# First stage of a two-layer diffusion backbone: block 3's shift formed on TensorE, small loads issued by ScalarE, products of zeros in two early waits of TensorE

## The chip, the cores and the metric

The kernel runs on one core of one Trainium2 chip. The time is the device time of one execution in microseconds (us). Of the kernel before, three runs are given, and one more execution was recorded by the profiler. The core's engines are named as the profile names them: PE (TensorE, matrix products), DVE (VectorE), ACT (ScalarE), POOL (GpSimd) and SP (SyncE, which only issues loads). Each takes its instructions in the order of the program and waits for others by semaphores.

## The reference, cut to what matters

A latent stream of 256 tokens and a context of 256 tokens, both 2048 wide, go through two layers; the change touches the beginning of the first, in which the input is modulated and keys and values are formed:

```python
sh1, sc1, g1, sh2, sc2, g2 = ada_params(c[:, None, :], ada_w[i], ada_b[i])   # silu(c) @ ada_w + ada_b, six parts
a = modulate(h, sh1, sc1)                                                     # h * (1 + sc1) + sh1
csh1, csc1, ... = ada_params(c_ctx, ada_w[i], ada_b[i])                       # the same for the context
ac = modulate(hc, csh1, csc1)
...
q, k, v = jnp.split(a @ w_qkv, 3, axis=-1)
```

So scale and shift, 2048 numbers each for latent and for context, are themselves products of a vector with a 2048 x 2048 matrix, and they are needed before the first product of the layer. All is fp32.

## The kernel before

The 2048 channels are cut into 16 **blocks** of 128 (`kt` in the code). In the first stage a loop over the blocks (functions `fetch`, `dot`, `gather`, `modulate`, `keys`, `values`) does for each block: load its two 128 x 2048 pieces of the modulation matrix (1 MB each: scale, then shift), its 128 x 512 of the transposed input (`xt`) and its 896 columns of key and value weights (`rkv`); form scale and shift; modulate; and add the block's share to three heads of keys (`kps`) and to 512 columns of values (`vps`), which stay in PSUM for the whole stage.

Products of data are made from two parts, a rounded high part and the rest (`hi`, `lo`; `ah`, `al` for the input): ACT rounds (L93), DVE subtracts (L94), and `mm3` issues three products for one (L88, L89, L90): high by high, high by rest, rest by high. A block has nine of them for the keys and twelve for the values. From block 3 on, twelve further ones form early shares of four more heads (`eps`).

Scale and shift come about in two ways:

- On PE (`dot`): 16 products against `c_pad`, silu of `c` and `c_ctx` in a padded tile (L350), leave four partial rows in PSUM. `gather` has ACT copy them to `row` (L359), sums and turns them by a product with the selector `sel` (L362), and DVE adds the bias `badj` and writes `mod` (L364). In the trace each of these full fp32 products has two records, so 32 for one set of 16.
- On DVE (`dot_dve`), for the shift of the blocks from `DVE0` = 3 on: the piece is laid out the other way round, and two passes over 2048 columns with sums (L337), against silu of `c` in `c_bc` and of `c_ctx` in `cc_bc` (which borrows the tile `oT`), give both shifts, to which L340 adds the bias.

`modulate` is then two scaled copies on ACT (`tmp`, L374), and the split into `ah` and `al`.

What sets the order: `pin` (`keep_in_program_order`) fixes the order in which an engine's pinned instructions are issued; the rest is placed by a scheduler. PE works ahead: within block `kt` it makes the sets of 16 of block `kt + 2` (`dots(ahead)`, after the keys) and the selection of that block after half of the values. Block 3 is an exception: its sets are made at the end of block 1, its selection within the keys of block 2 (`rows(3)`).

Loads are issued by SP (big blocks) and ACT, each in its own order. The 1 MB pieces share four buffers: three in `st` and, for the shift of every odd block, the one of `gate`. A load waits until the last reader of its buffer is done, and those behind it wait with it. Eight semaphores are shared in turn by all loads of SP and ACT, so a load also waits until the one eight before it has landed.

At the start ACT issues `badj`, `ident` and `sel`, then loads its table and makes silu of `c_col`; DVE copies that to `c_pad`; SP loads `c_col` and the two rows of `c`, which POOL spreads to all partitions (`spread`, L82), and then the blocks.

Of the kernel before, what the change touches and what calls it, by code (L numbers as in the profile page):

```python
# [11 lines left out]
F32 = mybir.dt.float32  # L12
# [7 lines left out]
P = 128  # L20
# [20 lines left out]
ADA = 4  # L41
FETCH = 3
BUSY = 0.3
DVE0 = 3
W0 = HK0 * P + 512
EARLY = tuple((3 + 4 * g + h, h, 4 * g) for g in range(3) for h in range(4))
EN = 4
# [4 lines left out]
def hybrid_kernel(ctx: ExitStack, tc: tile.TileContext, i, out):  # L52
# [3 lines left out]
    outer = ctx.enter_context(tc.tile_pool(name="outer", bufs=1))  # L56

    c_col = outer.tile([P, KT, 2], F32, tag="ccol", name="c_col")
    nc.sync.dma_start(c_col, i["c_col"])
    badj = outer.tile([P, 2, 6, KT], F32, tag="badj", name="badj")  # L60
    nc.scalar.dma_start(badj, i["ada_b_col"])
    ident = outer.tile([P, P], F32, tag="ident", name="ident")
    nc.scalar.dma_start(ident, i["ident"])
    eps_t = outer.tile([P, 1], F32, tag="eps", name="eps_t")
    nc.gpsimd.memset(eps_t, EPS)
    warm = outer.tile([P, 1], F32, tag="warm", name="warm")
    S.activation(c_col, c_col, AF.Silu)
    for t in (SC1, SC2):
        V.tensor_scalar(badj[:, :, t, :], badj[:, :, t, :], 1.0, None, ALU.add)
    lncol = outer.tile([P, 4, 2, KT], F32, tag="lncol", name="lncol")  # L70
    cols = outer.tile([P, 2, 6, KT], F32, tag="cols", name="cols")
    cols2 = outer.tile([P, 2, 6, KT], F32, tag="cols2", name="cols2")
# [7 lines left out]
    def spread(dst, src):  # L80
        nc.sync.dma_start(dst[0:1, :], src[None, :])
        nc.gpsimd.partition_broadcast(dst, dst[0:1, :])  # L82
# [194 lines left out]
    with tc.tile_pool(name="attnX", bufs=1) as px, ExitStack() as late:  # L277
# [21 lines left out]
        with tc.tile_pool(name="st", bufs=1) as st:  # L299
# [11 lines left out]
            def fetch(kt):  # L311
# [2 lines left out]
                    held[kt, t] = load_st(src, f"ap{kt}{t}", 2 * kt + t)  # L314
                load_x(kt)

            c_pad = st.tile([P, KT, 32], F32, tag="cpad", name="c_pad")
            nc.gpsimd.memset(c_pad, 0.0)
            V.tensor_copy(c_pad[:, :, 0:2], c_col)
            sel = st.tile([P, 2], F32, tag="sel", name="sel")  # L320
            nc.scalar.dma_start(sel, i["sel"])
            mod = st.tile([P, 2, KT, 2], F32, tag="mod", name="mod")
            kps = [stp_pool.tile([P, 512], F32, tag=f"k{h}", name=f"kps{h}") for h in range(HK0)]
            vps = [stp_pool.tile([P, 512], F32, tag=f"v{b}", name=f"vps{b}") for b in range(4)]
# [30 lines left out]
            def gather(kt):  # L355
                ps = dps.pop(kt)
                ts = 1 if kt >= DVE0 else 2
                row = st.tile([P, 2 * P], F32, tag="row", name=f"row{kt}", bufs=1)
                S.copy(row[:, 0 : ts * P], ps[:, 0 : ts * P])  # L359
                o = ps[:, 256:260].rearrange("p (t b) -> p t b", t=2)  # L360
                for t in range(ts):
                    pin(T.matmul(o[:, t, :], row[:, t * P : (t + 1) * P], sel, start=True, stop=True))  # L362
                for t, ada in enumerate((SC1, SH1)[:ts]):
                    V.tensor_scalar(mod[:, t, kt, :], o[:, t, :], badj[:, 0, ada, kt : kt + 1], None, ALU.add)  # L364
# [5 lines left out]
            def modulate(kt):  # L370
                tmp = st.tile([P, 512], F32, tag="tmp", name=f"tmp{kt}", bufs=2)
                for b in range(2):
                    sl = slice(b * 256, (b + 1) * 256)
                    S.activation(  # L374
                        tmp[:, sl], xt[kt][:, sl], AF.Identity,
                        bias=mod[:, 1, kt, b : b + 1], scale=mod[:, 0, kt, b : b + 1],
                    )
                split_into(ah[:, kt, :], al[:, kt, :], tmp)

            for n, bc in enumerate((c_bc, cc_bc)):  # L380
                spread(bc, i["c_rows"][n])
            fetch(0)
            prefetch(1)
            fetch(1)
            for t in range(2):
                dot(0, t)
            gather(0)
            modulate(0)
            for kt in range(KT):
                hi, lo = piece()  # L390
# [22 lines left out]
                keys(0)  # L413
                if kt == 2:
                    rows(3)
                keys(1)
                keys(2)
                dots(ahead)
# [14 lines left out]
                for at, h, k0 in EARLY:  # L433
                    if at == kt:
# [8 lines left out]
                        else:  # L443
                            free = NH - 2 * (h - HK0 + 1)
                            early[h] = oT[:, free : free + 2, :].rearrange("p a b -> p (a b)")
                            V.tensor_copy(early[h], ps)
                if 1 < kt and kt + 1 < KT:
                    modulate(kt + 1)
            nc.sync.dma_start(lncol, i["ln_col"])
        pa = late.enter_context(tc.tile_pool(name="attnA", bufs=1))  # L450
# [589 lines left out]
```

## Time and profile before

| | us |
|---|---|
| three runs: lowest, median, highest | 2460.63, 2462.59, 2463.62 |
| the profiled execution | 2464.19 |
| its span, first to last instruction | 2462.4 |
| PE, PE's weight loads, DVE, ACT, POOL busy | 2388.5, 1979.4, 1753.7, 1120.5, 110.3 |
| mean granted clock of TensorE | 0.991 of full |

The profiled execution's own time is 1.8 us over its span. In the profile a line such as L350 is the line of the kernel printed above; names of tiles stand without their numbers, output before input; "x32" counts instructions of one kind that follow each other; what stands behind "<-" in square brackets is who ended the idle time before the instruction. A view of busy times can be asked for any stretch, and it gives the granted clock of TensorE for it, 1.00 or less.

### The profile page before, as it was taken

The page shows a single profiled execution, that of the slowest core. Times are in us where ns is not written, and L with a number is a line of the kernel's source. Part 1 is how long each engine was busy: PE and PEld are TensorE (multiplying, and loading weights), DVE is VectorE, ACT ScalarE, POOL GpSimd, SP SyncE. Part 2 cuts the span into 40 slices and gives each one's busy share as a digit, 9 for nine tenths or more (in the row PEclk, how much of TensorE's full clock was granted, in tenths as well). Part 3 has the DMA queues.
Part 4 walks back from the last instruction along what each step waited for, and adds up shares of the span by engine and source line. Part 5 has one row for each costly group of instructions (what it writes and reads, how often), then busy time and mean ns, then how long its engine had stood idle before and what let it go on. Part 6 is the DMA issues. An engine that isn't in the chain of part 4 may idle for free. (4 is left out here: it accounts for less than half of the span.)

```text
span 2462.4 us, 31266 instructions
## 1 busy us (share of the span) xinstructions
PE 2388.5 (97%) x11574; PEld 1979.4 (80%) x11574; DVE 1753.7 (71%) x2158; ACT 1120.5 (46%) x1534; POOL 110.3 (4%) x54
## 2 busy tenths in 40 slices
PE   7999999999999999999999999899999999999998
PEld 5788888888788888887888778777888888888886
DVE  4878877777887777666778778778755555566666
ACT  3344434335554444443455554445544444445453
POOL 0000200000010010000000010020100000020000
PEclk9999999999999999999999999999999999999999
DMA  9978787877578888887888767766567676766563
GB/s 358 346 248 266 254 288 260 273 253 246 188 241 284 293 280 299 284 290 275 280 290 283 247 208 263 241 210 196 199 229 229 226 227 225 230 198 190 178 211 131
DMA packets 167682, 610.63 MB, mean 248 GB/s; under 512 B 19076, under 2 KB 21572, under 8 KB 163172
## 3 DMA queue, kind: packets, MB, share of 16 engines
q1 hardware_dynamic: 120888, 440.64, 53.9%
q10 hardware_dynamic: 46512, 167.96, 19.9%
q8 instruction: 90, 1.47, 0.2%
q14 instruction: 64, 0.52, 0.1%
q0 software_dynamic: 128, 0.03, 0.0%
HBM read 606.46 MB, written 2.10 MB: 247 GB/s over the span
## 5 line engine op out<-in xcount | busy, mean ns | idle before, releaser
L93 ACT CAST hwf<-rwf 128x1024 fp32r<-128x1024 f32 x320 | 336.9, 1053 | 491.2 <-PE pu L90 206.0
L94 DVE TENSOR_TENSOR lwf<-rwf,hwf 128x1024 fp32r<-128x1024 f32 x320 | 404.3, 1277 | 173.8 <-ACT hwf L93 172.8
L152 DVE SCALAR_TENSOR_TENSOR ad<-ad,c_bc 128x1024 f32<-128x1024 f32 x192 | 234.0, 1222 | 168.9 <-DMA ad<-in_ada_t 168.3
L88 PE MATMUL pod<-hwd,ghd 128*128 128x512 f32 x684 | 267.3, 391 | 3.5 <-DVE sg L815 3.5
L90 PE MATMUL pod<-hwd,gld 128*128 128x512 f32 x684 | 266.5, 390 | 0.7 <-DVE gld L94 0.7
L89 PE MATMUL pod<-lwd,ghd 128*128 128x512 f32 x684 | 266.8, 390 | 0.0
L176 DVE SCALAR_TENSOR_TENSOR gate<-ag,c_col,gate 128x1024 f32<-128x1024 f32 x128 | 164.4, 1288 | 121.1 <-DMA ag<-in_ada_g 120.8
L94 DVE TENSOR_TENSOR lwd<-rwd,hwd 128x1024 fp32r<-128x1024 f32 x172 | 211.7, 1232 | 51.3 <-ACT hwd L93 51.0
L93 ACT CAST hwd<-rwd 128x1024 fp32r<-128x1024 f32 x172 | 180.3, 1049 | 33.3 <-PE pu L90 11.5
L88 PEld LDWEIGHTS pod<-hwd,ghd 128*128 128x128 f32 x684 | 128.7, 188 | 30.5 <-DVE sg L815 4.0
L90 PEld LDWEIGHTS pod<-hwd,gld 128*128 128x128 f32 x684 | 128.7, 188 | 28.1 <-DVE gld L94 1.2
L89 PEld LDWEIGHTS pod<-lwd,ghd 128*128 128x128 f32 x684 | 128.8, 188 | 26.6
L88 PE MATMUL pg<-hwf,f1h 128*128 128x512 f32 x320 | 126.4, 395 | 0.0
L88 PE MATMUL pg<-hwf,f0h 128*128 128x512 f32 x320 | 126.4, 395 | 0.0
L90 PE MATMUL pg<-hwf,f1l 128*128 128x512 f32 x320 | 124.7, 390 | 0.0
L90 PE MATMUL pg<-hwf,f0l 128*128 128x512 f32 x320 | 124.7, 390 | 0.0
L88 PE MATMUL pu<-hwf,f0h 128*128 128x512 f32 x320 | 124.5, 389 | 0.0
L89 PE MATMUL pu<-lwf,f0h 128*128 128x512 f32 x320 | 124.5, 389 | 0.0
L90 PE MATMUL pu<-hwf,f0l 128*128 128x512 f32 x320 | 124.5, 389 | 0.0
L88 PE MATMUL pu<-hwf,f1h 128*128 128x512 f32 x320 | 124.5, 389 | 0.0
L89 PE MATMUL pu<-lwf,f1h 128*128 128x512 f32 x320 | 124.5, 389 | 0.0
L90 PE MATMUL pu<-hwf,f1l 128*128 128x512 f32 x320 | 124.5, 389 | 0.0
(338 smaller groups left out, 5345.1 us busy)
## 6 DMA issues: line engine op xcount, KB each, us to landing
rwf<-in_w_in_t SPq DMA_DIRECT2D x320, 512.0 KB
ad<-in_ada_t ACTq DMA_DIRECT2D x192, 512.0 KB
rwd<-in_w_out SPq DMA_DIRECT2D x176, 512.0 KB
ag<-in_ada_g ACTq DMA_DIRECT2D x128, 512.0 KB
rwg<-in_w_gin SPq DMA_DIRECT2D x64, 512.0 KB
ap<-in_ada_p SPq DMA_DIRECT2D x19, 1024.0 KB
rwq<-in_w_q SPq DMA_DIRECT2D x32, 512.0 KB
rwo<-in_w_o SPq DMA_DIRECT2D x32, 512.0 KB
```

Of the source, the lines that this page charges most:

```text
L88: keep(T.matmul(ps, sh, mh, start=first, stop=False))
L89: keep(T.matmul(ps, sh, ml, start=False, stop=False))
L90: keep(T.matmul(ps, sl, mh, start=False, stop=last))
L93: S.copy(hi, src)
L94: V.tensor_tensor(lo, src, hi.bitcast(F32), ALU.subtract)
L152: V.scalar_tensor_tensor(r, r, 1.0, c_bc[:, half * 1024 : (half + 1) * 1024], ALU.mult, ALU.mult, accum_out=o[:, nt : nt + 1],)
L176: V.scalar_tensor_tensor(g, loaded.pop(key), c_col[:, kt, 0:1], g, ALU.mult, ALU.add)
```

## The change

`DVE0` goes from 3 to 4, so the shift of block 3 is formed on PE like those of blocks 0 to 2, from a piece that is laid out as theirs; `modulate(3)` moves from the end of block 2 to right behind block 3's selection. At the start, `sel`, the bias in two halves (one for each layer), the two rows of `c` and `ident` are issued by ACT in a fixed order, behind its table load, and silu of `c` is written to `c_pad` by ACT; SP issues only `c_col` ahead of the blocks. `heat` puts products of a tile of zeros into PE's order: two 512 wide ahead of the first set of block 0, three 256 wide behind block 0's selection. They go to a PSUM tile whose first real product starts it anew.

```diff
--- before.py
+++ after.py
@@ -41,7 +41,7 @@
 ADA = 4
 FETCH = 3
 BUSY = 0.3
-DVE0 = 3
+DVE0 = 4
 W0 = HK0 * P + 512
 EARLY = tuple((3 + 4 * g + h, h, 4 * g) for g in range(3) for h in range(4))
 EN = 4
@@ -56,17 +56,13 @@
     outer = ctx.enter_context(tc.tile_pool(name="outer", bufs=1))
 
     c_col = outer.tile([P, KT, 2], F32, tag="ccol", name="c_col")
-    nc.sync.dma_start(c_col, i["c_col"])
+    tc.keep_in_program_order(nc.sync.dma_start(c_col, i["c_col"]))
     badj = outer.tile([P, 2, 6, KT], F32, tag="badj", name="badj")
-    nc.scalar.dma_start(badj, i["ada_b_col"])
     ident = outer.tile([P, P], F32, tag="ident", name="ident")
-    nc.scalar.dma_start(ident, i["ident"])
     eps_t = outer.tile([P, 1], F32, tag="eps", name="eps_t")
     nc.gpsimd.memset(eps_t, EPS)
     warm = outer.tile([P, 1], F32, tag="warm", name="warm")
-    S.activation(c_col, c_col, AF.Silu)
-    for t in (SC1, SC2):
-        V.tensor_scalar(badj[:, :, t, :], badj[:, :, t, :], 1.0, None, ALU.add)
+    tc.keep_in_program_order(S.activation(warm, eps_t, AF.Silu))
     lncol = outer.tile([P, 4, 2, KT], F32, tag="lncol", name="lncol")
     cols = outer.tile([P, 2, 6, KT], F32, tag="cols", name="cols")
     cols2 = outer.tile([P, 2, 6, KT], F32, tag="cols2", name="cols2")
@@ -314,11 +310,15 @@
                     held[kt, t] = load_st(src, f"ap{kt}{t}", 2 * kt + t)
                 load_x(kt)
 
+            zero = st.tile([P, 512], F32, tag="zero", name="zero")
+            nc.gpsimd.memset(zero, 0.0)
             c_pad = st.tile([P, KT, 32], F32, tag="cpad", name="c_pad")
             nc.gpsimd.memset(c_pad, 0.0)
-            V.tensor_copy(c_pad[:, :, 0:2], c_col)
             sel = st.tile([P, 2], F32, tag="sel", name="sel")
-            nc.scalar.dma_start(sel, i["sel"])
+            pin(nc.scalar.dma_start(sel, i["sel"]))
+            pin(nc.scalar.dma_start(badj[:, 0], i["ada_b_col"][:, 0]))
+            pin(S.activation(c_pad[:, :, 0:2], c_col, AF.Silu))
+            pin(S.activation(c_col, c_col, AF.Silu))
             mod = st.tile([P, 2, KT, 2], F32, tag="mod", name="mod")
             kps = [stp_pool.tile([P, 512], F32, tag=f"k{h}", name=f"kps{h}") for h in range(HK0)]
             vps = [stp_pool.tile([P, 512], F32, tag=f"v{b}", name=f"vps{b}") for b in range(4)]
@@ -378,13 +378,26 @@
                 split_into(ah[:, kt, :], al[:, kt, :], tmp)
 
             for n, bc in enumerate((c_bc, cc_bc)):
-                spread(bc, i["c_rows"][n])
+                pin(nc.scalar.dma_start(bc[0:1, :], i["c_rows"][n][None, :]))
+                nc.gpsimd.partition_broadcast(bc, bc[0:1, :])
+            pin(nc.scalar.dma_start(badj[:, 1], i["ada_b_col"][:, 1]))
+            pin(nc.scalar.dma_start(ident, i["ident"]))
+            for layer in range(2):
+                for t in (SC1, SC2):
+                    V.tensor_scalar(badj[:, layer, t, :], badj[:, layer, t, :], 1.0, None, ALU.add)
+
+            def heat(n, width):
+                for _ in range(n):
+                    pin(T.matmul(vps[3][:, :width], zero[:, :P], zero[:, :width], start=True, stop=True))
+
+            heat(2, 512)
             fetch(0)
             prefetch(1)
             fetch(1)
             for t in range(2):
                 dot(0, t)
             gather(0)
+            heat(3, 256)
             modulate(0)
             for kt in range(KT):
                 hi, lo = piece()
@@ -413,6 +426,7 @@
                 keys(0)
                 if kt == 2:
                     rows(3)
+                    modulate(3)
                 keys(1)
                 keys(2)
                 dots(ahead)
@@ -444,7 +458,7 @@
                             free = NH - 2 * (h - HK0 + 1)
                             early[h] = oT[:, free : free + 2, :].rearrange("p a b -> p (a b)")
                             V.tensor_copy(early[h], ps)
-                if 1 < kt and kt + 1 < KT:
+                if 2 < kt and kt + 1 < KT:
                     modulate(kt + 1)
             nc.sync.dma_start(lncol, i["ln_col"])
         pa = late.enter_context(tc.tile_pool(name="attnA", bufs=1))
```

Three places in the order of the instructions. First, **ACT at the beginning of the program**. Before (names are those of the text; a number behind one counts tiles):

```order
L61 DMA badj<-in_ada_b_col 128x192
L63 DMA ident<-in_ident 128x128
L321 DMA sel<-in_sel 128x2
L67 ACT_TABLE_LOAD
L67 ACTIVATE c_col<-c_col 128x32
L359 COPY row_155<-aps_122 128x256
L93 CAST hkv_0_112<-rkv_0_110 128x896
```

and now:

```order
L65 ACT_TABLE_LOAD
L65 ACTIVATE warm<-eps_t 128x1
L318 DMA sel<-in_sel 128x2
L319 DMA badj<-in_ada_b_col 128x96
L320 ACTIVATE c_pad<-c_col 128x16x2
L321 ACTIVATE c_col<-c_col 128x32
L381 DMA c_bc<-in_c_rows 1x2048
L381 DMA oT<-in_c_rows 1x2048
L383 DMA badj<-in_ada_b_col 128x96
L384 DMA ident<-in_ident 128x128
L359 COPY row_163<-aps_130 128x256
L89 CAST hkv_0_120<-rkv_0_118 128x896
```

The table load has moved ahead of all loads, which have the silus between them, and there are six loads in place of three ahead of block 0's row and weights (`row`, `hkv`).

Second, **DVE in blocks 2 and 3**, from the scale of block 3 (`mod<-aps`) to the shift of block 4 (the second `mod<-raw_c` before, the only one now). Before:

```order
L364 TENSOR_SCALAR mod<-aps_322,badj 128x2
L337 SCALAR_TENSOR_TENSOR junk_339,raw_c<-ap_318,oT 128x2048
L337 SCALAR_TENSOR_TENSOR ap_318,raw_c<-ap_318,c_bc 128x2048
L94 TENSOR_TENSOR lkv_0_346<-rkv_0_343,hkv_0_345 128x896
L340 TENSOR_SCALAR mod<-raw_c,badj 128x2
L94 TENSOR_TENSOR lwe_0_0_352<-rwe_0_0_349,hwe_0_0_351 128x512
L94 TENSOR_TENSOR al<-tmp_411,ah 128x512
L337 SCALAR_TENSOR_TENSOR junk_391,raw_c<-ap_370,oT 128x2048
L364 TENSOR_SCALAR mod<-aps_374,badj 128x2
L337 SCALAR_TENSOR_TENSOR ap_370,raw_c<-ap_370,c_bc 128x2048
L94 TENSOR_TENSOR lkv_0_419<-rkv_0_416,hkv_0_418 128x896
L340 TENSOR_SCALAR mod<-raw_c,badj 128x2
```

and now:

```order
L364 TENSOR_SCALAR mod<-aps_333,badj 128x2 x2
L90 TENSOR_TENSOR lkv_0_369<-rkv_0_366,hkv_0_368 128x896
L90 TENSOR_TENSOR lwe_0_0_375<-rwe_0_0_372,hwe_0_0_374 128x512
L90 TENSOR_TENSOR al<-tmp_387,ah 128x512
L364 TENSOR_SCALAR mod<-aps_404,badj 128x2
L337 SCALAR_TENSOR_TENSOR junk_421,raw_c<-ap_400,oT 128x2048
L337 SCALAR_TENSOR_TENSOR ap_400,raw_c<-ap_400,c_bc 128x2048
L90 TENSOR_TENSOR lkv_0_444<-rkv_0_441,hkv_0_443 128x896
L340 TENSOR_SCALAR mod<-raw_c,badj 128x2
```

The two passes for block 3 and their bias are gone, `mod` of block 3 is written twice (scale and shift) from PSUM, and the first pass for block 4 stands behind block 4's scale, where before it stood ahead of it.

Third, **ACT in blocks 2 and 3**: `row` of blocks 3, 4 and 5, with what stands between them. Before:

```order
L359 COPY row_358<-aps_322 128x128
L93 CAST hkv_0_345<-rkv_0_343 128x896
L93 CAST hwe_0_0_351<-rwe_0_0_349 128x512
L374 ACTIVATE tmp_411<-xt_320,mod 128x256 x2
L93 CAST ah<-tmp_411 128x512
L359 COPY row_401<-aps_374 128x128
L93 CAST hkv_0_418<-rkv_0_416 128x896
L374 ACTIVATE tmp_494<-xt_372,mod 128x256 x2
L359 COPY row_464<-aps_437 128x128
L93 CAST ah<-tmp_494 128x512
```

and now:

```order
L359 COPY row_381<-aps_333 128x256
L89 CAST hkv_0_368<-rkv_0_366 128x896
L89 CAST hwe_0_0_374<-rwe_0_0_372 128x512
L374 ACTIVATE tmp_387<-xt_331,mod 128x256 x2
L89 CAST ah<-tmp_387 128x512
L359 COPY row_431<-aps_404 128x128
L89 CAST hkv_0_443<-rkv_0_441 128x896
L374 ACTIVATE tmp_519<-xt_402,mod 128x256 x2
L359 COPY row_489<-aps_462 128x128
L89 CAST ah<-tmp_519 128x512
```

Before, `tmp` and `ah` of block 3 (the first `tmp`) stand ahead of block 4's `row`, and `tmp` of block 4 ahead of block 5's. The order of the kinds is the same now, with `tmp` of block 3 fed by a selection in place of DVE's passes; its `row` is 256 wide.

## The prediction

> **What bounds the kernel now.** I read the page first, then the busy time by stretches, then the waits of the first 60 us, then the timeline there. TensorE (PE) is busy for 2388.5 of 2462.4 us (the table above), so only a stage where it stands still can give anything. Of the stretches of 10 us at the start, this is the first that is full:
>
> ```profile
> 50.00:60.00 10.00, 10.00 (x72) 7.84 (x70) 7.53 (x12) 3.45 (x6) 0.00 (x0) 0.98 0.92 344
> ```
>
> (stretch, its length, then busy us and count of PE, PE's weight loads, DVE, ACT, POOL; granted clock; DMA share; GB/s). From 50 us on PE has no hole in this stage, so the change can only win before that. Two waits of PE in the view of waits of 0 to 60 us are what its parts aim at, the second in one piece of 3.8:
>
> ```profile
> PE aps L350 <- DMA ap<-in_ada_p: 8.1, 2, 7.6
> PE aps L362 <- ACT row L359: 4.3, 2, 3.8
> ```
>
> The second is best seen in the timeline (start us, length us, engine, line, what):
>
> ```profile
> 36.89 2.28 DVE L337 SCALAR_TENSOR_TENSOR junk<-ap,oT 128x2048 bf16<-128x2048 f32 x1
> ...
> 42.43 0.22 DVE L340 TENSOR_SCALAR mod<-raw_c,badj 128x2 f32<-128x2 f32 x1
> ...
> 42.69 1.09 ACT L374 ACTIVATE tmp<-xt,mod 128x256 f32<-128x256 f32 x2 [5.65 <-DVE mod L340]
> ...
> 44.34 0.26 ACT L359 COPY row<-aps 128x128 f32<-128x128 f32 x1
> ...
> 44.65 0.59 PE L362 MATMUL aps<-sel,row 128*128 128x2 f32 x2 [3.83 <-ACT row L359]
> ```
>
> PE has the products of block 4's scale and wants its row copied. ACT has done with that row nothing yet, because `tmp` of block 3 stands ahead of it, and `tmp` waits for block 3's shift, which DVE forms by two passes of 2.28 us (L337). The wait costs more than itself, as stretches of 3.41 us, cut where the granted clock changes, show:
>
> ```profile
> 16.27:19.68 3.41, 3.41 (x9) 2.48 (x8) 0.16 (x1) 0.00 (x0) 0.00 (x0) 1.00 1.05 426
> 40.16:43.57 3.41, 0.66 (x3) 0.19 (x1) 3.08 (x5) 0.88 (x2) 0.00 (x0) 1.00 0.57 171
> 43.57:46.99 3.42, 2.34 (x7) 1.96 (x8) 2.53 (x2) 0.99 (x3) 0.00 (x0) 0.50 0.97 384
> 46.99:50.40 3.41, 3.41 (x10) 2.64 (x9) 3.41 (x6) 0.94 (x1) 0.00 (x0) 0.50 0.99 374
> ```
>
> After a stretch with 0.66 us of work the clock is granted by half for two stretches. The first one of these has 2.34 us of work and does not end it; the second, full, does. At the start of the program no grant is on record yet, but the full stretch 16.27:19.68 holds 9 products and the half-clocked 46.99:50.40 holds 10: the same slow pace.
>
> **Block 3's shift goes to TensorE.** What it adds to PE is one more set of 16 products and one more selection; two sets and one, and two selections and one, stand in the timeline:
>
> ```profile
> 28.96 1.95 PE L350 MATMUL aps<-ap,c_pad 128*32 128x128 f32 x64
> ...
> 32.34 0.50 PE L362 MATMUL aps<-sel,row 128*128 128x2 f32 x4
> ...
> 38.14 1.08 PE L350 MATMUL aps<-ap,c_pad 128*32 128x128 f32 x32
> ...
> 53.69 0.28 PE L362 MATMUL aps<-sel,row 128*128 128x2 f32 x2
> ```
>
> So 0.87 + 0.22 = 1.1 us more on PE, at a place where PE is full. It takes 4.6 us of L337 from DVE, and `modulate(3)` now stands before block 4's row on ACT with its inputs there in time. The wait of 3.83 and the half clock behind it go. What is late next? By the new order DVE forms block 4's shift only behind block 4's scale, and ACT puts block 5's row behind block 4's `tmp`. That is the same queue of waits, one block on. Its length from one selection on PE to the next follows from these rows, with those above:
>
> ```profile
> 54.01 0.22 DVE L364 TENSOR_SCALAR mod<-aps,badj 128x2 f32<-128x2 f32 x1
> ...
> 55.30 0.39 PE L88 MATMUL eps<-ah,hwe 128*128 128x512 f32 x1
> ...
> 58.02 0.39 PE L88 MATMUL kps<-ah,hkv 128*128 128x512 f32 x1
> ...
> 61.68 0.26 ACT L359 COPY row<-aps 128x128 f32<-128x128 f32 x1
> ...
> 62.66 0.28 PE L362 MATMUL aps<-sel,row 128*128 128x2 f32 x2
> ...
> 62.98 0.22 DVE L364 TENSOR_SCALAR mod<-aps,badj 128x2 f32<-128x2 f32 x1 [0.48 <-PE aps L362]
> ```
>
> Selection to `mod` 0.32 (53.69 to 54.01), `mod` 0.22, from the first L337 to `tmp` 5.80 (36.89 to 42.69), `tmp` 1.1, row to selection 0.31: 7.7 us. PE's own way between the two selections is a block's 8.97 (53.69 to 62.66) without the 12 early products, which take 2.72 (55.30 to 58.02) and stand behind block 5's selection: 6.25. So a **new wait of about 1.4 us** on PE at block 5's selection. Its bounds: nothing, if DVE gets through 1.4 sooner, and 3.1, if the clock falls again for one stretch (half of 3.41 more). I take 1.4, as 1.4 in 3.41 leaves 2.0 of work, and the stretch that lost the clock had 0.66. From there on the rows are block by block as before. DVE arrives late once more, since `al` of block 4 stands ahead of the next `mod`; it had 0.48 to spare in each block (the last row), so I count 0.3 and then nothing.
>
> Sum, from the start of block 3's products (34.27 in the timeline) to block 5's selection. Before: 53.69 - 34.27 = 19.4. After, on PE: two sets 1.9, nine key products with the pause behind them 2.3 (a row below shows 2.04 for eight), two selections 0.5, one set 1.1, six value products 1.4 (half of the twelve early ones), so 7.2 to block 4's selection; then 7.7 of the chain: 14.9, and 0.3: 15.2. **Gain 4.2 us.**
>
> **The start.** The two rows of `c` leave SP's queue, so its first big block is issued earlier; the zero products go into PE's two waits; the small loads go to ACT's queue, behind the table load. What the path is now, and the same place once warm:
>
> ```profile
> 1.20 0.33 SPq L81 DMA_DIRECT2D c_bc<-in_c_rows  x1
> ...
> 1.84 0.83 SPq L306 DMA_DIRECT2D ap<-in_ada_p  x2
> ...
> 10.05 1.94 PE L350 MATMUL aps<-ap,c_pad 128*32 128x128 f32 x32 [0.49 <-DMA ap<-in_ada_p]
> ...
> 15.76 0.79 PE L88 MATMUL kps<-ah,hkv 128*128 128x512 f32 x1 [2.27 <-ACT ah L93]
> ...
> 16.49 0.79 PE L89 MATMUL kps<-al,hkv 128*128 128x512 f32 x1
> ...
> 20.00 1.96 PE L350 MATMUL aps<-ap,c_pad 128*32 128x128 f32 x64
> ...
> 26.92 0.50 PE L89 MATMUL kps<-al,hkv 128*128 128x512 f32 x1 [0.22 <-DVE al L94]
> ```
>
> The first issue moves from 1.84 to 1.20, so 0.64 earlier, if nothing on the way slows. From the second product of the keys to the next block's L350 it takes 3.51 now (16.49 to 20.00) and 2.04 warm (26.92 to 28.96): 1.47 for the clock. Together at most 2.1. A zero product of full fp32 is dearer than its neighbours; nearest is this group:
>
> ```profile
> L881 PE MATMUL sp<-vv,ws 128*128 128x256 f32 x32 | 9.7, 402 | 5.0 <-DVE u L882 5.0
> ```
>
> It has two records a product, 0.4 us each with the latency of a lone record in it. Three of 256 columns are six such records, at most 2.4 warm and 4.8 cold, in the wait of 2.27 before the keys: they run over by 0 to 2.5. I take 0, since records that follow each other hide the latency and the clock turns up on the way; at the other end the keys start at 17.6. The first two, twice as wide, are 1.6 to 6.4 us from about 1.4 on, over before the second block's products, and cost nothing.
>
> [...]
>
> Against this stands what the small loads meet. Before, they ran ahead of the big blocks; one did not quite, as the timeline shows (with POOL's second broadcast, and two of DVE's steps for block 0):
>
> ```profile
> 0.74 0.41 ACTq L61 DMA_DIRECT2D badj<-in_ada_b_col  x1
> ...
> 1.67 0.46 ACTq L321 DMA_DIRECT2D sel<-in_sel  x1
> ...
> 2.16 1.28 ACT L67 ACT_TABLE_LOAD   x1 [2.16 <-issue]
> ...
> 2.88 0.27 DVE L69 TENSOR_SCALAR badj<-badj 128x32 f32<-128x32 f32 x2 [2.88 <-DMA badj<-in_ada_b_col]
> ...
> 3.79 1.69 DVE L319 COPY c_pad<-c_col 128x32 f32<-128x32 f32 x1 [0.64 <-ACT c_col L67]
> ...
> 5.31 2.32 POOL L82 PARTITION_BROADCAST oT<-oT  x1
> ...
> 6.87 0.33 SPq L368 DMA_DIRECT2D xt<-in_xcT  x1
> ...
> 13.85 1.08 DVE L94 TENSOR_TENSOR lkv<-rkv,hkv 128x896 fp32r<-128x896 f32 x1
> ...
> 15.74 0.69 DVE L94 TENSOR_TENSOR al<-tmp,ah 128x512 fp32r<-128x512 f32 x1 [0.81 <-ACT ah L93]
> ```
>
> and SP's own waits:
>
> ```profile
> SPq L368 <- DMA sel<-in_sel: 1.7, 1, 1.7
> ```
>
> `badj`, issued first, was there 2.1 us later (0.74 to 2.88, when DVE starts on it); `sel`, 1 KB, released SP's `xt` at 6.87, so it took 5.2 us in company of the blocks. Now all of them start at 2.3 at the soonest (from 0.74 the table load of 1.28, then `warm`) and run in that company, one behind the other. Between 2.1 and 5.2 each, I take 2.6 for each behind `sel`: `sel` at 7.5, the first half of `badj` at 10, the rows of `c` by 10.5, the second half of `badj` near 13. Needed are `badj` at PE's first selection, near 12 (in time), and its second half before `lkv` on DVE (by 13.5, just in time). But POOL's two broadcasts, 2.3 us each, now run to about 15 where they ended at 7.63, and DVE's copy of 32 columns to `c_pad` shows what that can do: it lasted 1.69 and ended as the second broadcast came up at 5.31 (5.48). So `lkv` (1.08) and `al` (0.69) come behind 15, and the second key product, which needs `al`, at about 16.9, against 16.49 before. With the warm 2.04 behind it, block 1's products start at 18.95 for 20.00: **gain 1.0**, of at most 2.1; the other end is a loss of 1.2 (0.6 later still, and the clock lost in that wait).
>
> [...]
>
> All else moves along: `ident`, first used by the transposes of attention, after this stage; the second memset on POOL; SP's loads of block 5, which no longer wait for DVE's passes. DMA is no bound (344 GB/s in the full stretch against 426 at the start).
>
> **Rivals.** (1) *The start wins in full*: the small loads land sooner and `al` is there at 15.8; gain 2.1 + 4.2. For it: PE's wait for `ah` ends near 15.1. Against: the 5.2 us of `sel`. (2) *The start gives it back*: the first half of `badj` or ACT's queue, held by the issue of `ident`, is late; loss 1.2 against the 4.2; the same if the change does not warm PE at all and the wait at block 5 halves the clock. (3) *Slower*: DVE becomes the bound of the stage. If the chain of block 5 comes 0.9 late and does not catch up, each of the 12 blocks behind pays 0.9, 10.8 in all; it decides from the point where the chain between two selections is longer than 8.97. Against: DVE works 7.5 of 10 us and has 0.48 to spare a block. (4) The new wait is not there, gain 1.4 more; only if DVE's order let it start earlier, which it does not; within rival 1's time.
>
> **How the numbers follow.** The profiled execution took 2464.19, the median shown is 2462.59. Against the first: 2464.19 - 4.2 - 1.0 = 2459.0. It lies 1.6 above the median, and two stretches of half clock behind the wait are the long case (where they fall is chance), which the other runs need not have; I take 0.6 of that off: **2458.4**, 45%. Rival 1 by the same way 2457.3, with (4) 2455.9: 30%. Rival 2: 2464.19 - 4.2 + 1.2 - 0.6 = 2460.6: 20%. Rival 3: 2462.6 - 4.2 + 10.8 = 2469.2: 5%. Range 2455.0 to 2462.0: it takes in the first three with the spread of the runs shown (3 us) and leaves the last out. A difference under 0.2% (4.9 us) cannot be told from none in this kernel; the forecast lies just inside that, so most of rival 1 and a third of my own case count as faster: faster 0.40, same 0.55, slower 0.05.
>
> **What would show it.** Right: no half clock between 40 and 50 us; at block 5's selection (near 48 us) a wait of PE for ACT's row of 1 to 2 us, behind DVE's L340; keys from 15 to 16 us at 0.23 apart; L94 `al` of block 0 behind POOL's broadcast. Wrong: a wait at every block's selection after 60 us, half clock at 17 or 48 us, or holes later in the program that grow by what the first stage won.

## The result, and the profile after

| | before | changed |
|---|---|---|
| median of 13 runs each, us | 2462.59 | **2447.53** |
| lowest to highest, us | 2456.14 to 2466.52 | 2441.26 to 2458.58 |
| ratio of the times, 95% interval | | 0.995 (0.9934 to 0.9967) |
| profiled execution, us | 2464.19 | 2458.32 |
| its span, us; granted clock | 2462.4; 0.991 | 2456.5; 0.991 |

By the medians the change makes the kernel 15 us faster, by the means, which the ratio compares, 12 (2462.04 and 2449.83); 2458.4 was forecast, with a range of 2455.0 to 2462.0. One run of `late6`, an experiment below, took 6524.85 us at a granted clock of 0.494, and the numbers of `late6` are those of the other eleven. The profiled execution of the changed kernel (2458.32) is one of the slowest of its 13 runs, and by chance almost the forecast. It may be read for the first stage, which hardly varies, and not for where the rest of the gain lies.

The waits of PE over the whole program of the changed kernel, the two that the change aimed at and a new one (who waits for whom: us in total, times, longest):

```profile
PE aps L350 <- DMA ap<-in_ada_p: 2.6, 2, 1.6
PE aps L362 <- ACT row L359: 1.6, 2, 1.1
...
PE aps L350 <- DVE oT L460: 0.3, 1, 0.3
```

The first two were 8.1 and 4.3 in all. The 7.6 us in front of the first product are not gone but filled, as the timeline of the changed kernel shows (start us, length us, engine, line, what):

```profile
0.74 1.28 ACT L65 ACT_TABLE_LOAD   x1 [0.74 <-PEq L1044]
...
0.88 0.39 ACTq L318 DMA_DIRECT2D sel<-in_sel  x1
1.18 0.89 SPq L302 DMA_DIRECT2D ap<-in_ada_p  x2
...
1.35 3.78 PE L391 MATMUL vps<-zero 128*128 128x512 f32 x4 [1.35 <-POOL zero L314]
...
2.72 0.48 ACTq L381 DMA_DIRECT2D c_bc<-in_c_rows  x1
...
6.70 1.93 PE L350 MATMUL aps<-ap,c_pad 128*32 128x128 f32 x32 [1.57 <-DMA ap<-in_ada_p]
...
9.85 2.30 POOL L382 PARTITION_BROADCAST oT<-oT  x1
...
12.93 2.91 PE L391 MATMUL vps<-zero 128*128 128x256 f32 x6
...
15.33 0.69 DVE L90 TENSOR_TENSOR al<-tmp,ah 128x512 fp32r<-128x512 f32 x1 [0.66 <-ACT ah L89]
15.35 0.91 PE L84 MATMUL kps<-ah,hkv 128*128 128x512 f32 x1
16.08 0.79 PE L85 MATMUL kps<-al,hkv 128*128 128x512 f32 x1
...
17.66 0.39 PE L86 MATMUL kps<-ah,lkv 128*128 128x512 f32 x1
17.89 0.39 PE L84 MATMUL kps<-ah,hkv 128*128 128x512 f32 x1
...
18.66 1.61 PE L350 MATMUL aps<-ap,c_pad 128*32 128x128 f32 x49
```

Block 1's products stand at 18.66 where they stood at 20.00. Further on, the selections of blocks 4 and 5 (same view), and three stretches of 3.41 us, as long as those in the prediction, from a view by stretches (bounds, length, busy us and count of PE, PE's weight loads, DVE, ACT, POOL; granted clock; DMA share; GB/s):

```profile
40.06 0.28 PE L362 MATMUL aps<-sel,row 128*128 128x2 f32 x2
...
46.07 0.22 DVE L340 TENSOR_SCALAR mod<-raw_c,badj 128x2 f32<-128x2 f32 x1
...
47.61 0.38 PE L362 MATMUL aps<-sel,row 128*128 128x2 f32 x2 [1.14 <-ACT row L359]
...
57.13 0.28 PE L362 MATMUL aps<-sel,row 128*128 128x2 f32 x2
```

```profile
40.57:43.98 3.41, 3.41 (x23) 2.57 (x25) 3.38 (x4) 0.95 (x1) 0.00 (x0) 1.00 0.97 396
43.98:47.40 3.42, 2.49 (x38) 1.69 (x30) 2.31 (x4) 1.08 (x3) 0.00 (x0) 1.00 1.05 415
47.40:50.81 3.41, 3.20 (x15) 2.67 (x16) 2.70 (x3) 1.30 (x4) 0.00 (x0) 1.00 1.02 422
```

The forecast comes true here: no wait at block 4's selection, a new one of 1.14 us at block 5's behind DVE's L340, and no half clock. Block 6's selection stands at 57.13 for 62.66: 5.5 us won. It is still 5.5 where attention begins. This is the first row of the products of `qps` in a view by tile (line, engine, operation, count: least/median/longest ns, first to last start in us), of the kernel before and of the changed one:

```profile
L88 PEld LDWEIGHTS qps<-ah,hwq x256: 186/192/337, 160.8 to 574.0; 128*128 128x128 f32 x128
```

```profile
L84 PEld LDWEIGHTS qps<-ah,hwq x256: 186/192/337, 155.3 to 575.5; 128*128 128x128 f32 x128
```

It is gone by the end of attention (574.0 and 575.5): in this execution DVE waits for a load there and PE for DVE, 4.18 us where the kernel before has 1.68, and a stretch of half clock follows (waits in the timeline, before and changed, and the stretch in the changed kernel):

```profile
198.92 0.50 PE L89 MATMUL vps<-lwv,ah 128*128 128x512 f32 x1 [1.68 <-DVE lwv L94]
```

```profile
191.89 1.28 DVE L172 SCALAR_TENSOR_TENSOR gate<-ag,c_col,gate 128x1024 f32<-128x1024 f32 x1 [3.12 <-DMA ag<-in_ada_g]
196.16 0.79 PE L85 MATMUL vps<-lwv,ah 128*128 128x512 f32 x1 [4.18 <-DVE lwv L90]
```

```profile
194.80:201.60 6.80, 5.44 (x19) 4.86 (x20) 5.50 (x8) 0.77 (x2) 0.00 (x0) 0.50 0.62 201
```

So the first stage wins 5 to 6 us, and the median 15. The order of the instructions behind the first stage is the same in both kernels on every engine, so the question is where the other 8 to 10 us come from.

### The profile page after: what moved, and what is told of

Same layout as the page of the kernel before. It is cut to its first block, busy times and chain, and to the rows that moved or that the text cites. A ratio compares the mean times of both kernels' runs of the same rounds, so it can differ in the third digit from the quotient of the medians.

```text
span 2456.5 us, 31360 instructions
## 1 busy us (share of the span) xinstructions
PE 2391.5 (97%) x11618; PEld 1982.4 (81%) x11618; DVE 1748.4 (71%) x2155; ACT 1121.9 (46%) x1536; POOL 115.2 (5%) x55
## 5 line engine op out<-in xcount | busy, mean ns | idle before, releaser
L172 DVE SCALAR_TENSOR_TENSOR gate<-ag,c_col,gate 128x1024 f32<-128x1024 f32 x128 | 165.2, 1294 | 115.2 <-DMA ag<-in_ada_g 115.0
```

The source lines that it names most:

```text
L172: V.scalar_tensor_tensor(g, loaded.pop(key), c_col[:, kt, 0:1], g, ALU.mult, ALU.add)
```

## The experiments

The theories, by the letters that the expectations use. **F**: only the first stage counts; later stages are the same work, and differences there are chance. **L**: what the later stages win hangs on reaching them earlier, since the loads of SP's and ACT's queues then meet PE otherwise. The other letters are told in the expectations where they first stand. In all, two numbers are compared: the median, and the time **behind attention's start**, which is the median less the start of `qps` in the profiled execution. Such a number is uncertain by some 3 to 6 us, half the width of the intervals of the ratios, and it joins the median of many runs with the start in one; the start of attention itself moves little (160.8, 162.4, 161.7 and 161.7 in four profiled runs with the first stage of before, and 154.6 to 155.8 in five with that of the changed kernel).

| kernel | median us (runs) | ratio to before, 95% | attention starts | behind it |
|---|---|---|---|---|
| before | 2462.59 (13) | | 160.8 | 2301.8 |
| before_again | 2465.80 (12) | 1.0007 (0.9988 to 1.0026) | 162.4 | 2303.4 |
| split | 2465.23 (12) | 0.9997 (0.9978 to 1.0017) | 161.7 | 2303.5 |
| block3 | 2452.41 (12) | 0.9963 (0.9949 to 0.9977) | 157.8 | 2294.6 |
| start | 2455.69 (12) | 0.9973 (0.9956 to 0.9989) | 158.3 | 2297.4 |
| heat | 2455.73 (12) | 0.9964 (0.9946 to 0.9981) | 158.2 | 2297.5 |
| noheat | 2454.53 (12) | 0.9964 (0.9943 to 0.9985) | 156.4 | 2298.1 |
| changed | 2447.53 (13) | 0.9950 (0.9934 to 0.9967) | 155.3 | 2292.2 |
| after_again | 2447.99 (6) | 0.9936 (0.9913 to 0.9959) | 154.9 | 2293.1 |
| after_pad | 2449.77 (10) | 0.9941 (0.9921 to 0.9960) | 155.3 | 2294.5 |
| whole | 2448.94 (10) | 0.9933 (0.9908 to 0.9958) | 155.8 | 2293.1 |
| late6 | 2458.96 (11) | 0.9982 (0.9965 to 0.9999) | 165.6 | 2293.4 |
| late13 | 2463.26 (12) | 0.9999 (0.9983 to 1.0015) | 169.7 | 2293.6 |
| before_late6 | 2469.03 (12) | 1.0008 (0.9989 to 1.0026) | 171.8 | 2297.2 |
| before_i116 | 2463.06 (12) | 0.9991 (0.9973 to 1.0010) | 166.6 | 2296.5 |
| after_i256 | 2462.27 (12) | 0.9986 (0.9972 to 1.0001) | 167.3 | 2295.0 |

The kernel before ran beside each group of these, and the ratios are to those runs; its medians there were 2462.89 (`after_again`, `before_again`, `block3`, `start`), 2462.93 (`late6`, `late13`, `after_pad`, `noheat`), 2464.85 (the cut kernels), 2463.95 (`split`, `whole`, `heat`, `before_late6`) and 2466.80 (`before_i116`, `after_i256`).

**Both kernels again, and each half of the change alone.** `after_again` and `before_again` have no edit.

> The changed kernel once more, for a second trace and more times. Theory F (all of the gain is made in the first stage, the rest is chance from one execution to the next): the first product of qps starts near 155.3 us as in the first trace (160.8 before), the stages behind it last as long as before within some us either way, and the median is 5 us below the kernel before. Theory L (loads of the later stages meet PE otherwise because they start earlier): qps near 155.3 too, but attention (from the first product of qps to the first of powo, 413.6 us before) or the gMLP (from the first of gv to the first of pogo, 201.6 before) shorter by about 10 together, and the median 10 to 15 us below.

> The kernel before once more, for a second trace of it: says how much of a stage's length is chance. F: attention and gMLP differ from the first trace (413.6 and 201.6 us) by as much as those of the changed kernel do from one trace to the next, some 5 us. L: they stay within 2 us of the first trace. The time is that of the kernel before within 3 us.

`block3` is the kernel before with these edits, `start` the changed kernel without them:

```
-DVE0 = 3
+DVE0 = 4
...
                     rows(3)
+                    modulate(3)
...
-                if 1 < kt and kt + 1 < KT:
+                if 2 < kt and kt + 1 < KT:
```

> Block 3's part alone (DVE0 = 4, modulate(3) behind its selection), the start as before. By the prediction's sum the first product of qps comes 4.2 us sooner than 160.8, at 156.6, with a wait of about 1.4 us at block 5's selection in place of the 3.8 at block 4's, and no half clock at 43 us. F: the time is 4.2 us below before. L: the time falls by more than that, since what the later stages answer to is how early they begin.

> The start's part alone (loads on ACT's queue, zero products), with block 3's shift on DVE as before. By the prediction's sum qps comes 1.0 us sooner (between 2.1 sooner and 1.2 later) than 160.8; the wait of 3.8 at block 4's selection is still there. F: the time is 1 us below before, which cannot be told from none. L: below before by more than 3 us if the order in which the small loads land is what the later stages answer to.

The gain is there again (2447.99) and the kernel before has not moved (2465.80, and 2462.89 beside it). The halves give 10 and 7 us beside 2462.89, where attention starts 4 and 3 us earlier than the 161.7 of the first stage of before in the mean of four profiled runs:

```profile
L88 PEld LDWEIGHTS qps<-ah,hwq x256: 186/192/337, 157.8 to 574.0; 128*128 128x128 f32 x128
```

That is `block3`. The halves add up to 18 us, the whole to 15, and each wins at least as much behind the first stage as in it. By their intervals `block3` wins 5.7 to 12.6 us and `start` 2.7 to 10.8: F's 4 lies outside the first, F's 3 just inside the second. The whole change wins 8.1 to 16.3, where F has 5 to 6: **F falls**. The sign that L gave for `after_again` does not show either: there attention and the gated MLP, as its expectation bounds them, last 414.9 and 198.8 us, and in the two runs of the kernel before 413.6 and 201.6, 412.3 and 199.1.

**Reaching attention later, another layout, no zero products.** `late6` and `late13` are the changed kernel with 7 and 14 times this product behind the loop over the blocks:

```
+            hold = stp_pool.tile([P, 512], F32, tag="a", name="hold")
+            for _ in range(7):
+                pin(T.matmul(hold, zero[:, :P], zero, start=True, stop=True))
             nc.sync.dma_start(lncol, i["ln_col"])
```

> The changed kernel with 7 zero products of 512 columns on PE behind the first stage, in front of attention: about 6.6 us more, so that attention is reached when the kernel before reaches it (161 to 162 us; the changed kernel 155). Theory F (only the first stage counts, the later stages lose or win by chance): 2447.7 + 6.6 = 2454.3. Theory L (what the later stages won, some 8 us, hangs on reaching them earlier): the later stages are as in the kernel before, about 2462. Theory B (the layout of the inputs in DRAM or of the program makes the later stages faster, not the time): 2454.3, with the later stages as short as in the changed kernel.

> As the run before, with 14 zero products: 13.2 us more. F and B: 2447.7 + 13.2 = 2460.9, a slope of one. L: 2468 or more, a slope of two up to the old arrival and one behind it.

`after_pad` and `noheat`:

```
-    a["ada_s"] = np.stack([... for kt in range(DVE0, KT)])
+    a["ada_s"] = np.stack([... for kt in range(DVE0 - 1, KT)])
...
-                    src = i["ada_s"][kt - DVE0] if t and kt >= DVE0 else i["ada_p"][kt, t]
+                    src = i["ada_s"][kt - DVE0 + 1] if t and kt >= DVE0 else i["ada_p"][kt, t]
```

```
-            heat(2, 512)
...
-            heat(3, 256)
```

> The changed kernel with a thirteenth block in front of the stack of shift weights that DVE reads (never loaded), so that this input has its old length and all inputs behind it lie 1 MB further on, as in the kernel before. F and L: 2447.7, no difference. B (layout): 4 us more or more, about 2452.

> The changed kernel without the zero products. F: the keys of block 0 run at the slow clock again (0.73 instead of 0.23 us apart, 1.5 us in all), and the first pieces of the second set too: the first stage ends 1.5 to 2 us later, 2449.5. L: twice that, 2451.5. If the zero products cost more than they bring (they are about 6.7 us of PE work): less than 2447.

The delay of `late6` came out longer than planned, since behind the zero products PE had to wait for DVE's `kl` (timeline of `late6`):

```profile
165.58 0.55 PE L84 MATMUL qps<-ah,hwq 128*128 128x256 f32 x1 [4.83 <-DVE kl L90]
```

10.3 us later than the changed kernel it begins attention, and it takes 11.4 more; `late13` begins 14.4 later and takes 15.7 more. Behind the start of attention both take what the changed kernel takes (2293.4 and 2293.6), though they get there after the kernel before does. That speaks against L, but these two and `before_late6` below differ in one thing more: the scheduler placed the beginning of attention in another order, on PE, DVE, ACT and SP. On PE the order is that of the other kernels only from the 397th of the 10448 records behind attention's start on; SP issues its first loads of `bias` at 148.08 in the changed kernel, ahead of two of `rwq`, and at 160.81 in `late6`, behind them. So it is by `before_i116` and `after_i256` at the end, whose order behind the first stage is that of the kernels they come from, that **L falls**: they reach attention 5 and 6 us later than the kernel before, and take 2296.5 and 2295.0 from there. It is not the earlier start. `after_pad` loses 2 of 15 us, within its interval: **B falls** for that input. `noheat` loses 7, where its first stage loses 1.1 (156.4 for 155.3): more than either number given ahead of it, though its interval (2449 to 2459) takes both in.

**How long the first stage is, and where the gain stands at the gated MLP.** The cut kernels end early:

```
         stp.close()
+        for n in range(2):
+            for b in range(2):
+                ...
+                pin(nc.sync.dma_start(out[b * P : (b + 1) * P, sl], r))
+        late.close()
+        return
```

> The kernel before, cut off behind its first stage: everything from attention on is left out, and the output is a copy of the residual input. It gives the length of the first stage over many runs instead of two profiled ones (attention begins at 160.8 and 162.4 there), so about 163 to 168 us. Its difference to the changed kernel cut at the same place counts: F: 6 to 7 us (160.8 and 162.4 against 155.3, 154.9 and 155.3), so that some 8 of the 14.6 us come from later stages. Theory T (the first stage of the kernel before is often longer than the two profiled runs show): 10 to 14 us.

> The changed kernel, cut off behind its first stage like the run before; all behind it is left out. F: 6 to 7 us below that run; T: 10 to 14 us below it.

```
     ffn(0, m, (0, G2), "d0", begin, free)
+    for b in range(2):
+        nc.sync.dma_start(out[b * P : (b + 1) * P, :], h_t[:, b, :])
+    return
```

> The kernel before, cut off behind the first feed-forward network (in front of the gated MLP, which starts at 1413.9 and 1416.0 in the profiled runs); the gated MLP and the second feed-forward network are left out, the output is the residual there. About 1420 to 1430 us. Its difference to the changed kernel cut at the same place counts: if all of the gain is there by then, 14 to 15; if the gain grows evenly over the later stages, 10 to 11; if attention and the first network win nothing beyond the first stage, 6 to 7; if they lose (the three profiled runs of the changed kernel begin the gated MLP at 1413.3, 1404.6 and 1413.1), 5 or less.

> The changed kernel, cut off in front of the gated MLP like the run before, with the same parts left out. Below that run by 14 to 15, 10 to 11, 6 to 7, or 5 or less, as told there.

Cut behind the first stage: 166.47 (165.59 to 166.93 in four of six runs, 168.30 and 169.28 in the others) and 163.21 (162.49 to 163.85 in four of five, 165.20 in the other). The difference of 3.3 is smaller than either number expected; PE's last product of the stage ends at 159.35 and 154.16 in the two profiled runs, 5.2 apart, and the copy of the output, which ends these programs, does not end with PE (the spans are 165.2 and 161.5). But no run of the first stage of before is longer than the others by 5 us or more: **T falls**. Cut in front of the gated MLP: 1431.60 (1425.93 to 1433.15) and 1418.79 (1416.00 to 1421.27), four runs each: 12.8 us. Their attentions start at 161.7 and 154.6, 7.1 apart. By that, about 6 of the extra 8 to 10 us lie in attention and the first feed-forward network, and the rest behind. The profiled executions of whole programs place them otherwise. In the mean of `before`, `before_again` and `split`, and of the thirteen others, attention lasts 415.4 and 417.2 us, from the first product of `powo` to that of `gv` it is 839.7 and 836.7, the gated MLP lasts 199.0 and 196.1, and the rest 846.5 and 844.9. So where the extra us lie is not settled.

One place stands out in the profiled runs, the second product of that network, where PE waits for DVE's tile `sg`. `before_again` and `after_again`, from the waits of PE:

```profile
PE pod L88 <- DVE sg L815: 5.3, 2, 4.8
```

```profile
PE pod L84 <- DVE sg L829: 1.3, 1, 1.3
```

In total it is 3.5, 5.3, 2.5 and 4.3 in before, `before_again`, `split` and `block3`, and in the twelve other runs of whole programs 0 (three times), 1.1, 1.3, 1.4, 1.4, 2.2, 3.4, 3.6, 3.6 and 4.2, which is 1.9 in the mean. That is 2 us, and with the half clock behind a long one some more: in before it is granted from 1170.00 to 1173.41, behind the wait of 3.54 that ends at 1168.63. It does not single out the kernel before (`block3`, `after_pad`).

**Which edit carries it.** One difference between the kernels was still untested, the load of the bias in two pieces:

```
-    nc.scalar.dma_start(badj, i["ada_b_col"])
+    for n in range(2):
+        nc.scalar.dma_start(badj[:, n], i["ada_b_col"][:, n])
```

That is `split`, an edit of the kernel before. `whole` is the changed kernel with the reverse edit.

> The kernel before with the load of badj in two halves, on the same queue at the same place, nothing else. It adds one DMA, so every later DMA uses the next of the eight semaphores. Theory D (that turn, or one DMA more, is what the later stages feel): 4 to 8 us below the kernel before, 2455 to 2459. F and all others: no difference, 2462.9 within 2.

> The changed kernel with badj loaded in one piece, at the place of its first half: the DMA semaphores stand again as in the kernel before. D: 4 to 8 us of the gain are lost, 2452 to 2456. Otherwise: 2447.7 within 2; the first stage may move by half a microsecond, since the rows of c are loaded behind 96 KB instead of 48.

`heat` is the kernel before with `zero`, `heat(2, 512)` and `heat(3, 256)` of the change and nothing else; `before_late6` is the kernel before with `zero` and the seven products of `late6`.

> The kernel before with the zero products alone, at the same two places. By the first stage (F): the pause before the keys (2.3 us) is filled and the clock is up, 1.2 to 1.5 us less, 2461.5. Theory Z (the zero products are worth more than that, as the 6.8 us between the changed kernel and the one without them say): 2456 to 2458.

> The kernel before with 7 zero products of 512 columns behind the first stage, as in late6; that run reached attention 10.5 us later than the changed kernel and took 9.6 longer in the mean. F and D: the same 10 us more than the kernel before, 2472 to 2473. Theory W (any small move of the first stage's end against the loads brings the later stages to the shorter time; the kernel before is the odd one): 2462 to 2466.

**D falls** on both sides: 2465.23 and 2448.94, and the intervals (2458.5 to 2468.1 and 2441.3 to 2453.6) reach into D's ranges only with their last 2 us. `heat` alone gives what `start` gives (2455.73 and 2455.69): the moved loads are worth nothing that these runs can measure. Its first stage wins about 3 us (158.2), not 1.2 to 1.5, and the half clock shows why (stretches of `heat`):

```profile
40.47:43.88 3.41, 0.86 (x5) 0.78 (x6) 2.19 (x5) 1.88 (x4) 0.00 (x0) 1.00 0.93 332
43.88:47.29 3.41, 3.41 (x10) 2.62 (x9) 3.41 (x4) 0.94 (x1) 0.00 (x0) 0.51 1.02 377
47.29:50.71 3.42, 3.42 (x43) 2.54 (x42) 1.93 (x4) 1.46 (x4) 0.00 (x0) 0.99 0.97 353
```

One stretch of half clock in place of two: the wait of block 4 (3.71 us) ended at 43.02, in the stretch with 0.86 us of work, where that of before ended at 44.65, 1.08 us into the stretch behind the one with 0.66. Behind attention's start `heat` still wins 5 (1 to 10 by its interval), with the same instructions in the same order there. And `before_late6`, which has the first stage of before and reaches attention 10 us later, takes 5 us more than the runs of before beside it in the median, and by its interval at most 6.4 (0.0026 of 2464): it wins about 5 behind that start as well, with the other order at the beginning of attention told above. That speaks for **W**.

**The instruction packets.** The page has a DMA queue of instructions, with 90 packets before, where TensorE has 11574 records, and 91 in the changed kernel, where it has 11618 (queue, kind: packets, MB, share):

```profile
q8 instruction: 90, 1.47, 0.2%
```

```profile
q8 instruction: 91, 1.49, 0.3%
```

A packet has 16 KB (1.47 MB in 90). If the queue is TensorE's, it holds some 257 instructions, by 2 x 11574 records of PE in 90 packets, and the runs take it as 256: both are the author's estimate, and by it records that are added in front move all later packets against the loads. The two runs that follow were to move the packets alone:

```
-            heat(2, 512)
-            heat(3, 256)
+            heat(29, 2)
```

(`before_i116`, an edit of `heat`)

```
-            heat(2, 512)
+            heat(44, 2)
```

(`after_i256`, an edit of the changed kernel)

> The kernel before with 29 zero products of 2 columns on PE in its first wait (it waits 7.6 us there for the first block), nothing else: 116 PE instructions more, as in late6 against the kernel before. Their time lies in that wait, so the first stage ends at 160 to 161.5 as before. Theory I (where the instruction packets fall among the loads sets the later stages): the later stages are some 9 us shorter, 2452 to 2456. All other theories: no difference, 2463 within 2.

> The changed kernel with its first two zero products of 512 columns replaced by 44 of 2 columns: 168 PE instructions more, 256 more than the kernel before, so that each packet falls again where it falls there (one packet earlier). The first stage should end at 154 to 155 as in the changed kernel, half a microsecond later at most. I: the later stages are those of the kernel before, 2455 to 2458. All others: 2448 within 2.

Narrow products were not short. A group of `before_i116` in the first 20 us, and attention's start in it:

```profile
L386 PE MATMUL vps<-zero 128*128 128x2 f32 x58 | 12.5, 352 | 1.4 <-POOL zero L318 1.4
```

```profile
L88 PEld LDWEIGHTS qps<-ah,hwq x256: 186/192/337, 166.6 to 582.9; 128*128 128x128 f32 x128
```

12.5 us for 58 records, against a wait of 7.6: the first stage ends some 5 us late, and in `after_i256` 12. So the medians do not test what they were to test, but the times behind attention's start do. `before_i116` takes 2296.5, 5 to 7 less than the kernel before (2 to 12 by its interval, beside the runs of before in its group): as I wants it, and W too. `after_i256` has its packets where before has them (in the packet records the one ahead of `pod`'s first product stands 5.5 us ahead of it; 5.4 in before, 16.7 in the changed kernel), and takes 2295.0, not 2302 (by its interval it wins 5 to 13 behind that start): **I falls** in this form.

## Why the prediction was wrong

**Point by point.** (1) The wait of 3.83 and the half clock behind it are gone: right. (2) A new wait of about 1.4 at block 5's selection, behind L340, and 0.3 later: 1.14 and 0.3 (`aps` L350 waits that long for DVE in the waits of the changed kernel). Right. (3) "Gain 4.2 us" for block 3: 62.66 - 57.13 = 5.5 less the start's 1.3 is 4.2. Right. (4) "Gain 1.0" for the start: 20.00 - 18.66 = 1.34; near by the sum, not by its reasons, so partly by luck. (The "loss of 1.2" at the other end is 1.0 by its own rows, 16.9 + 0.6 + 3.51 = 21.0 for 20.00, which changes nothing here.) The small loads were not behind the table load: `sel` was issued at 0.88, during it, and not at 2.3. The rows of `c` were there by 7.70, POOL was done at 12.15 and not near 15, and `al` (15.33, 0.69 us long) met no broadcast. That a broadcast holds `lkv` and `al` up, as the sum has it, is shown by no run: none has them beside one. So rival 1 was right on the loads. But the clock did not turn up where the sum has it: the first two products of the keys start 0.73 apart, as before, and only later ones 0.23. And `heat` has block 1's products at 18.38 with the old loads, so what was won here needs the zero products alone. That the first two buy nothing is seen in `whole`, the one execution of the changed start that has the clock on record from there (stretches):

```profile
1.56:4.98 3.42, 3.42 (x4) 0.97 (x4) 0.00 (x0) 1.12 (x4) 0.20 (x1) 1.00 0.83 248
4.98:8.39 3.41, 1.22 (x33) 0.84 (x32) 0.41 (x4) 0.00 (x0) 0.15 (x1) 1.00 1.01 414
8.39:11.80 3.41, 1.97 (x33) 1.42 (x33) 0.00 (x0) 0.47 (x2) 3.41 (x2) 0.50 1.06 429
```

A full stretch, then one with 1.22 us of work, in which the first set runs, then half clock when the second set comes.

**The step that failed** is the sentence "All else moves along", and with it the reading that "the change can only win before that": the sum has no term for what lies behind the first stage, though PE stands still for 57.5 us there (2301.6 less 2244.1 busy from attention's start on, in the profiled execution of before). The first stage won 5.5 us in the profiled pair and 6.5 in the mean of all profiled runs (161.7 to 155.2), where the terms gave 5.2. The median fell by 15.1. In its place the runs show that the 2300 us behind the first stage, with the same instructions in the same order, are not one number for all kernels: 2301.8 to 2303.5 in the kernel before and in `split`, and 2292.2 to 2298.1 in the thirteen others, whether they reach attention 6 us earlier or 10 us later (in `late6`, `late13` and `before_late6` with another order at its beginning). So the forecast of the first stage was right, and what it left out was larger. The last bound fell with it: the range counted the first stage's unknowns and the spread of the runs shown, and nothing for a shift of all that comes behind.

**What stays open.** Why the kernel before stands apart. Ruled out are the time at which attention is reached (`before_i116`, `after_i256`), the layout of the one input whose size changes (`after_pad`), the DMA semaphores (`split`, `whole`), a longer first stage than the profiles show (the cut kernels) and the place of TensorE's instruction packets alone (`after_i256`). The profiled executions say only what kind of time it is: behind attention's start the three of `before`, `before_again` and `split` last 2300.7 us in the mean and the thirteen others 2294.9; half of the difference is PE standing still (57.1 and 54.3), half the same products taking less time. Single ones overlap: the changed kernel's first lasts 2301.2. What all thirteen have and `split` has not is more products of PE in front of attention. A kernel that has it without taking time from PE was tried, and took time. That the kernel before sits at an unlucky place, from which any step wins 5 to 10 us, fits all rows, but it names no mechanism, and values that are uncertain by 3 to 6 us cannot tell the thirteen from each other.

## What to carry to other kernels

In a long program with many short waits behind its loads, what lies behind an edit can change by more than the edit itself is worth: here 8 to 10 us of 2300 against 5 to 6, for a reason that stays open. A forecast of a small change needs that in its range, and a gain of a few us is only an edit's own when the stage that it touches shows it; zero products somewhere else are the control to run, and one profiled execution (here one of the slowest of 13) shows stages, not medians.

## What the hardware showed

- ACT's queue issued DMAs while ACT loaded a table, in the changed kernel: `sel` at 0.88, with the load from 0.74 to 2.02.
- A zero product of full fp32 shrank far less than its columns: 0.215 us a record for 2 columns at the start (12.5 / 58, `before_i116`), against 0.95 for 512 there (3.78 / 4, the changed kernel), and 0.44 for 512 in `before_late6` later on (6.17 us for 14).
- The same wait of 3.7 to 3.9 us cost two stretches of half clock in before (3.83 us; 43.57 to 50.40 at 0.50), and one in `heat` (3.71; 43.88 to 47.29 at 0.51) and `start` (3.9; 44.10 to 47.50 at 0.51). In `heat` block 4's selection stands at 43.02, 1.6 us earlier than in before.
